# A decoder kernel's last microseconds: the final reciprocal root through ScalarE's square root, sums as one group, the last rows stored by column halves

## The chip, the core and the metric

The kernel runs on one core of a Trainium2 chip. The metric is the device time of one execution in microseconds (us); the value that counts is the median of several runs. Five engines work side by side, each through its own instructions in order: PE (TensorE, matrix products and transposes), DVE (VectorE), ACT (ScalarE), POOL (GpSimd) and SP (SyncE, which here only issues transfers). They wait for one another through semaphores. PE writes to PSUM, from which ACT and DVE read; the DMA engines carry data between SBUF and device memory.

## The reference

Two layers of a decoder trunk over 512 tokens of width 1024, in float32: layer 0 has a diagonal state-space mixer, layer 1 a short gated convolution, and each is followed by a SwiGLU feed-forward block of hidden width 2816. The end, which the change is about, is the last residual and a plain RMS norm:

```python
def rms_norm(x, g):
    x32 = x.astype(jnp.float32)
    y = x32 * lax.rsqrt(jnp.mean(x32 * x32, axis=-1, keepdims=True) + RMS_EPS)
    return (y * g.astype(jnp.float32)).astype(x.dtype)
...
        x = x + g2 * swiglu(h, w_ffn_in[i], w_ffn_out[i])
    return rms_norm(x, final_g)
```

## The kernel before

**Layout.** The activations stand transposed in `xT`: 128 partitions hold 128 of the 1024 channels, eight such blocks `k` lie side by side, and the free axis is the 512 tokens. Weights are split into a high part `wh` (rounded, copied by ACT) and a low part `wl` (the rest, by DVE or POOL), and every product is three matmuls: `wh` and `wl` by the high part of the activations, `wh` by the low part. The weights stream from device memory through SP's queue.

**Stages.** A state-space stage comes first (its instruction order is a table in the file), then the output projection of the mixer (`pre`, `half`, `glu`), the feed-forward block of layer 0, the convolution, the feed-forward block of layer 1, and the end. From the output projection on, the order is the order of the code, except that a scheduler moves an instruction forward on its engine when its operands and tiles are free early. In the output projection ACT and DVE turn the mixer's transposed result from PSUM (`ytp`) into the high and low parts `yT`, which `half` multiplies.

**The end.** The last product of layer 1 is done for the two halves of the tokens, `s=1` and then `s=2`, by `f1.tail`. For each half, `f1.fix` adds the residual into `xT` (DVE), squares it (ACT, `sq`) and adds the squares up over the channel blocks in `acc` (DVE); `fin_scale` multiplies by the final gain into `xg` (ACT); `fin_t` transposes `xg` back to rows of tokens in PSUM (`yt`, PE). `fin_sums` then sums `acc` over the partitions by matmuls against a column of ones (`ssq`, two row blocks `b` of 128 tokens) and calls `rsqrt_small`: an integer guess from the exponent and three Newton steps, 11 small DVE instructions on two columns of the tile `nst`. `fin_out` scales the rows by the result into `yo`: the left 512 columns on ACT, the right 512 on DVE; row block 0 is stored through SP's queue and row block 1 through ACT's, 512 KB each. For `s=1` all of this lies in `hook`, between the products of `s=2`; for `s=2` it is the end of the program. The last square of `s=2` isn't added into `acc`: it is summed by its own matmuls (`q`).

`rsqrt_small` is also used by the norms between the layers (`Norm.sums`).

Of the kernel before, what the change touches and what calls it, by code (L numbers as in the profile page):

```python
# [8 lines left out]
F32 = mybir.dt.float32  # L9
F32R = mybir.dt.float32r  # L10
I32 = mybir.dt.int32
AF = mybir.ActivationFunctionType
ALU = mybir.AluOpType
# [3 lines left out]
P = 128  # L17
D = 1024
# [7 lines left out]
EPS = 1e-6  # L26
# [235 lines left out]
def rsqrt_small(e, n, src, scale):  # L262

    h, y, t = e.nst[:, 0, 0:n], e.nst[:, 1, 0:n], e.nst[:, 2, 0:n]
    e.ts(h, src, scale / 2, EPS / 2, ALU.mult, ALU.add)
    e.ts(y.bitcast(I32), h.bitcast(I32), -0.5, float(0x5F3759DF - 0x80400000), ALU.mult, ALU.add)
    for _ in range(3):
        for c in range(n):
            q = slice(c, c + 1)
            e.stt(t[:, q], y[:, q], y[:, q], h[:, q], ALU.mult, ALU.mult)  # L270
        e.stt(y, t, 1.5, y, ALU.subtract, ALU.mult)
    return y


@with_exitstack
def hybrid_trunk(ctx: ExitStack, tc, x, c, norm1_g, norm2_g, w_ada, b_ada,
# [3 lines left out]
    e = common(tc, ctx)  # L280
    nc = tc.nc
    V, A, PE, SP = e.V, e.A, e.PE, e.SP
# [48 lines left out]
    SL = (slice(0, T), slice(0, TH), slice(TH, T))  # L331
# [39 lines left out]
    if 1:  # L371
# [35 lines left out]
        fp = ctx.enter_context(tc.tile_pool(name="fp", bufs=2))  # L407
        ws.wx = ctx.enter_context(tc.tile_pool(name="wx", bufs=Weights.EXTRA))

        def ft(tag, n=T, dt=F32):  # L410
            return fp.tile([P, n], dt, tag=tag, name=tag)

        accs = fp.tile([P, T], F32, tag="acc", bufs=1, name="acc")
# [21 lines left out]
        class Norm:  # L435
# [5 lines left out]
            def sums(self):  # L441
                self.ps = e.ps("ssq")
                o = (self.s - 1) * TH
                for b in range(2):
                    e.mm(self.ps[:, b:b + 1], accs[:, o + b * P:o + b * P + P], e.ones1[:, 0:1], True, True)
                self.y = rsqrt_small(e, 2, self.ps[:, 0:2], 1.0 / D)
# [238 lines left out]
        ov = out[0].rearrange("(c h j) d -> h c j d", h=2, j=4)  # L685
# [3 lines left out]
        def fin_scale(k, s):  # L689
            A.activation(out=rows(xg[s][:, k]), in_=rowsin(xT[:, k, SL[s]]), func=AF.Copy, scale=e.vec2[:, 24 + k:25 + k])  # L690
# [9 lines left out]
        def fin_out(n, s):  # L700
            for b in range(2):
                yo = e.slot([P, D], "yo")
                A.activation(out=yo[:, 0:512], in_=yt[(s, b, 0)], func=AF.Copy, scale=n.y[:, b:b + 1])
                V.tensor_scalar_mul(out=yo[:, 512:1024], in0=yt[(s, b, 1)], scalar1=n.y[:, b:b + 1])
                (SP if b == 0 else A).dma_start(out=ov[s - 1, b * 32:b * 32 + 32], in_=yo)

        def fin_sums(s, q=None):

            ps = e.ps("ssq")
            for b in range(2):  # L710
                cs = slice(b * P, b * P + P)
                e.mm(ps[:, b:b + 1], accs[:, SL[s]][:, cs], e.ones1[:, 0:1], True, q is None)
                if q is not None:
                    e.mm(ps[:, b:b + 1], q[:, cs], e.ones1[:, 0:1], False, True)
            n = Env()
            n.y = rsqrt_small(e, 2, ps[:, 0:2], 1.0 / D)
            return n

        for k in range(4):
            for s in (1, 2):  # L720
                fin_scale(k, s)
# [6 lines left out]
        def hook(j):  # L728
            if j == 0:
                n1.append(fin_sums(1))  # L730
                fin_t(1, range(KD))
            if j < 3:
                f1.fix(j, t2, 2)
                fin_scale(4 + j, 2)
            if j == 2:
                fin_out(n1[0], 1)
# [4 lines left out]
        q = ft("sq")[:, 0:TH]  # L741
        A.activation(out=rows(q), in_=rowsin(xT[:, 7, SL[2]]), func=AF.Square)
        fin_scale(7, 2)
        fin_t(2, range(7))
        n2 = fin_sums(2, q)
        fin_t(2, [7])
        fin_out(n2, 2)


# [745 lines left out]
```

## Time and profile before

| | |
|---|---|
| median of three runs | 1159.06 us (1158.73 to 1160.02) |
| the profiled execution | 1159.56 us |
| its span, first to last instruction | 1157.8 us |
| mean granted clock of PE | 0.986 |
| PE busy | 1105.8 us (96% of the span) |
| DVE busy | 643.7 us (56%) |
| ACT busy | 390.3 us (34%) |
| POOL busy | 180.7 us (16%) |

The 1.8 us between the span and the execution's own time lie before the first and behind the last instruction. The terms of the prediction are taken from the profiled execution; it is 0.5 us above the median.

In the timeline a row is: start in us, length in us, engine, line, operation, what is written from what, count, and in brackets how long the engine sat idle before it and who ended that. Rows of equal instructions that follow each other are merged; the length then runs from the first start to the last end. `SPq` and `ACTq` are what SP's and ACT's sequencers do, such as issuing a transfer. In the chain of work a row is start, length and work; `issue` is time for which nothing in the profile shows a cause.

### The profile page before, as it was taken

Reading aid. Unit: us, or ns where it says so; the run is one execution under the profiler, and the core shown is the slowest. Engines: PE = TensorE matmul, PEld = TensorE weight load, DVE = VectorE, ACT = ScalarE, POOL = GpSimd, SP = SyncE. Lnnn points to the kernel's source line nnn. Section 1 sums busy time; section 2 is a strip of 40 time slices with the busy share of each in tenths; the row PEclk is TensorE's granted clock in tenths of the full one; section 3 lists DMA queues with packets and bytes.
Section 4 is the critical chain, followed back from the end, with each engine's and each line's share of the span. In section 5 each row is a group of like instructions: output and inputs, shape, how many; then the busy total and the mean of one; then the engine's idle time right before and its main releaser. Section 6 shows DMA issues by size and latency. Waiting matters only on the chain.

```text
span 1157.8 us, 16329 instructions
## 1 busy us (share of the span) xinstructions
PE 1105.8 (96%) x6520; PEld 932.5 (81%) x6520; DVE 643.7 (56%) x1249; ACT 390.3 (34%) x596; POOL 180.7 (16%) x134
## 2 busy tenths in 40 slices
PE   4778999899999999999999999999999999999997
PEld 2567778898888888888889888899888888888886
DVE  8898323974666267734687666757334324243234
ACT  4744344442231132222334242334223113222244
POOL 4897817400000000000050000031000000000000
PEclk9889999899999999999999999999999999999999
DMA  9337654217894498726723939512332332332101
GB/s 280 126 115 259 201 184 128 91 55 182 194 195 120 119 194 196 182 91 137 173 92 100 207 113 209 154 58 89 110 110 80 103 109 78 104 109 92 63 28 73
DMA packets 141787, 153.50 MB, mean 133 GB/s; under 512 B 8224, under 2 KB 129164, under 8 KB 141712
## 3 DMA queue, kind: packets, MB, share of 16 engines
q1 hardware_dynamic: 140640, 150.79, 48.7%
q10 hardware_dynamic: 784, 1.58, 0.5%
q8 instruction: 51, 0.84, 0.3%
q0 software_dynamic: 288, 0.10, 0.1%
q14 instruction: 24, 0.20, 0.1%
HBM read 147.99 MB, written 2.10 MB: 130 GB/s over the span
## 4 chain that ended last, share of the span: by engine, by line
PE 85%; DVE 11%; ACT 2%; issue 1%; DMA 0%; DVEq 0%; ACTq 0%
PE o L117 79%; PE t L117 2%; DVE sx L109 1%; DVE scq L109 1%; DVE sg L109 1%; DVE hlo L115 1%; DVE xT L115 1%; PE gmm L117 1%; DVE acc L109 1%; PE yps L117 1%; DVE sr L120 0%; DVE v L109 0%; PE xtp L118 0%; ACT u L1229 0%; DVE scr L115 0%
## 5 line engine op out<-in xcount | busy, mean ns | idle before, releaser
L117 PE MATMUL o<-wide,wh 128*128 128x512 f32 (+1 forms) x992 | 364.2, 370 | 1.8 <-ACT wide L459 1.8
L117 PE MATMUL o<-wide,wl 128*128 128x512 f32 (+1 forms) x992 | 363.4, 369 | 0.0
L117 PE MATMUL o<-hlo,wh 128*128 128x512 f32 (+1 forms) x992 | 354.7, 370 | 2.3 <-DVE hlo L115 2.2
L119 ACT ACTIVATE wh<-wr 128x1024 fp32r<-128x1024 f32 (+1 forms) x184 | 188.6, 1039 | 387.0 <-PE o L117 305.1
L109 DVE TENSOR_TENSOR wl<-wr,wh 128x1024 fp32r<-128x1024 f32 (+1 forms) x156 | 184.8, 1195 | 157.8 <-ACT wh L119 156.0
L117 PEld LDWEIGHTS o<-wide,wh 128*128 128x128 f32 x992 | 187.6, 189 | 33.4 <-ACT wide L459 2.6
L117 PEld LDWEIGHTS o<-wide,wl 128*128 128x128 f32 x992 | 187.5, 189 | 30.8
L117 PEld LDWEIGHTS o<-hlo,wh 128*128 128x128 f32 x992 | 182.8, 189 | 34.8 <-DVE hlo L115 3.1
L117 PE MATMUL o<-hid,wh 128*128 128x512 f32 (+1 forms) x704 | 205.5, 375 | 0.0
L109 POOL TENSOR_TENSOR wl<-wr,wh 128x1024 fp32r<-128x1024 f32 x28 | 68.5, 2464 | 571.4 <-ACT wh L119 561.6
L117 PEld LDWEIGHTS o<-hid,wh 128*128 128x128 f32 x704 | 129.2, 188 | 23.8
L117 PE MATMUL o<-hid,wl 128*128 128x512 f32 (+1 forms) x352 | 131.8, 375 | 0.0
L109 DVE TENSOR_TENSOR sg<-sg,o 128x512 f32<-128x512 f32 (+1 forms) x50 | 31.8, 644 | 166.5 <-PE o L117 163.7
L115 DVE SCALAR_TENSOR_TENSOR aacc<-ada,cper,aacc 128x256 f32<-128x256 f32 x217 | 108.3, 499 | 19.1 <-DMA ada<-in_w_ada_dram 13.2
L515 ACT ACTIVATE sg<-o 128x512 f32<-128x512 f32 (+1 forms) x48 | 26.8, 562 | 170.0 <-PE o L117 168.4
L117 PEld LDWEIGHTS o<-hid,wl 128*128 128x128 f32 x352 | 66.3, 188 | 11.8
L117 PE MATMUL o<-yT,wh 128*128 128x512 f32 (+1 forms) x256 | 72.9, 366 | 0.0
L115 DVE SCALAR_TENSOR_TENSOR xT<-o,mod,xT 128x512 f32<-128x512 f32 (+1 forms) x56 | 38.6, 692 | 55.0 <-PE o L117 54.7
L117 PEld LDWEIGHTS o<-yT,wh 128*128 128x128 f32 x256 | 46.1, 189 | 8.1 <-issue 0.4
L117 PE MATMUL o<-yT,wl 128*128 128x512 f32 (+1 forms) x128 | 46.4, 363 | 0.0
L429 ACT ACTIVATE sq<-xT 128x256 f32<-128x256 f32 (+1 forms) x43 | 23.5, 550 | 50.8 <-DVE xT L115 47.3
L109 DVE TENSOR_TENSOR acc<-acc,sq 128x256 f32<-128x256 f32 (+1 forms) x40 | 26.1, 652 | 17.4 <-ACT sq L429 17.2
(222 smaller groups left out, 1031.4 us busy)
## 6 DMA issues: line engine op xcount, KB each, us to landing
wr<-in_w_ffn_in_dram SPq DMA_DIRECT2D x88, 512.0 KB, 3.6
ada<-in_w_ada_dram SPq DMA_DIRECT2D x112, 256.0 KB, 9.6
wr<-in_w_ffn_out_dram SPq DMA_DIRECT2D x40, 512.0 KB, 3.9
gt<-in_w_ada_dram SPq DMA_DIRECT2D x12, 1024.0 KB, 6.0
wr<-in_conv_w_in_dram SPq DMA_DIRECT2D x24, 512.0 KB, 3.6
aw<-in_w_ada_dram SPq DMA_DIRECT2D x16, 512.0 KB, 8.6
wr<-in_ssm_w_out_dram SPq DMA_DIRECT2D x16, 512.0 KB, 6.3
wr<-in_conv_w_out_dram SPq DMA_DIRECT2D x8, 512.0 KB, 6.1
```

Source lines behind the costliest of these rows:

```text
L109: (eng or e.V).tensor_tensor(out=out, in0=a, in1=b, op=op)
L115: e.stt = lambda o, a, s, b, op0, op1: e.V.scalar_tensor_tensor(out=o, in0=a, scalar=s, in1=b, op0=op0, op1=op1)
L117: e.mm = lambda o, l, r, start, stop: e.PE.matmul(out=o, lhsT=l, rhs=r, start=start, stop=stop)
L119: e.cp = lambda o, i: e.A.activation(out=o, in_=i, func=AF.Copy)
L429: A.activation(out=rows(q) if st.get("rows") else q, in_=rowsin(xT[:, k, SL[s]]) if st.get("rows") else xT[:, k, SL[s]], func=AF.Square)
L515: A.activation(out=w, in_=g[:, 0:width(s)], func=AF.Silu)
```

## The change

`fin_sums` calls a new function, `rsqrt_root`, in place of `rsqrt_small`. ACT takes the square root of the mean square plus epsilon, DVE computes `-(mean + eps)/2` and the reciprocal of ACT's root, and one Newton step of three DVE instructions follows. In the matmuls of the sums, the two row blocks form one accumulation group, and the order is both blocks of `acc`, then both of `q`. For `s=2` each row block leaves in two transfers of 256 KB: the left columns through ACT's queue, the right ones through SP's. At the start of the end's code a tile `eps` of one column is filled by DVE, and ACT takes one square root of it, into a spare column of `nst`.

```diff
+def rsqrt_root(e, n, src, scale):
+    h, y, t = e.nst[:, 0, 0:n], e.nst[:, 1, 0:n], e.nst[:, 2, 0:n]
+    e.A.activation(out=t, in_=src, func=AF.Sqrt, scale=scale, bias=e.eps)
+    e.ts(h, src, -scale / 2, -EPS / 2, ALU.mult, ALU.add)
+    e.V.reciprocal(out=y, in_=t)
+    for c in range(n):
+        q = slice(c, c + 1)
+        e.stt(t[:, q], y[:, q], y[:, q], h[:, q], ALU.mult, ALU.mult)
+    e.stt(y, t, 1.5, y, ALU.add, ALU.mult)
+    return y
...
-                (SP if b == 0 else A).dma_start(out=ov[s - 1, b * 32:b * 32 + 32], in_=yo)
+                if s == 1:
+                    (SP if b == 0 else A).dma_start(out=ov[s - 1, b * 32:b * 32 + 32], in_=yo)
+                else:
+                    for h, q in enumerate((A, SP)):
+                        hs = slice(h * 512, h * 512 + 512)
+                        q.dma_start(out=ov[s - 1, b * 32:b * 32 + 32, :, hs], in_=yo[:, hs])
 
         def fin_sums(s, q=None):
 
             ps = e.ps("ssq")
-            for b in range(2):
-                cs = slice(b * P, b * P + P)
-                e.mm(ps[:, b:b + 1], accs[:, SL[s]][:, cs], e.ones1[:, 0:1], True, q is None)
-                if q is not None:
-                    e.mm(ps[:, b:b + 1], q[:, cs], e.ones1[:, 0:1], False, True)
+            qs = [accs[:, SL[s]]] + ([] if q is None else [q])
+            for i, t in enumerate(qs):
+                for b in range(2):
+                    e.mm(ps[:, b:b + 1], t[:, b * P:b * P + P], e.ones1[:, 0:1], i + b == 0, i + b == len(qs))
             n = Env()
-            n.y = rsqrt_small(e, 2, ps[:, 0:2], 1.0 / D)
+            n.y = rsqrt_root(e, 2, ps[:, 0:2], 1.0 / D)
             return n
 
+        e.eps = fp.tile([P, 1], F32, tag="eps", bufs=1, name="eps")
+        V.memset(e.eps, EPS)
+        A.activation(out=e.nst[:, 2, 4:5], in_=e.eps, func=AF.Sqrt)
```

The scheduler moves the two instructions that fill `eps` and take its root. On ACT in the output projection of layer 0, far ahead of the end, stands before (`wh` and `wl` are weights, `yT` the mixer's result, `part` a partial product, `sg` the gate):

```order
131 L119 ACTIVATE wh_2108<-wr_2094 128x1024
132 L119 ACTIVATE wh_2086<-wr_2084 128x1024
133 L119 ACTIVATE yT_1981<-ytp 128x2x256 x2
134 L119 ACTIVATE part_2044<-o_1880 128x512
135 L119 ACTIVATE wh_2114<-wr_2100 128x1024
136 L119 ACTIVATE wh_2120<-wr_2106 128x1024
137 L119 ACTIVATE wh_2126<-wr_2112 128x1024
138 L572 ACT_TABLE_LOAD
139 L572 ACTIVATE sg<-o_1998 128x512
```

and now:

```order
131 L119 ACTIVATE wh_2108<-wr_2094 128x1024
132 L119 ACTIVATE wh_2086<-wr_2084 128x1024
133 L739 ACT_TABLE_LOAD
134 L739 ACTIVATE nst<-eps 128x1
135 L119 ACTIVATE yT_1981<-ytp 128x2x256 x2
136 L119 ACTIVATE part_2044<-o_1880 128x512
137 L119 ACTIVATE wh_2114<-wr_2100 128x1024
138 L119 ACTIVATE wh_2120<-wr_2106 128x1024
139 L119 ACTIVATE wh_2126<-wr_2112 128x1024
140 L586 ACT_TABLE_LOAD
141 L586 ACTIVATE sg<-o_1998 128x512
```

The root of `eps` and a load of the function table that it needs stand ahead of the two copies to `yT`; the load for the gate's function behind them was there before.

On PE, at the same place, stand in both kernels the last products by the first half of `yT` and the first ones by the part that these two copies write:

```order
471 L117 MATMUL o_1999<-yT_1447,wl_1898 128x512
472 L117 MATMUL o_1999<-yT_1448,wh_1897 128x512
473 L117 MATMUL o_1996<-yT_1981,wh_2086 128x512
474 L117 MATMUL o_1997<-yT_1981,wh_2086 128x512
475 L117 MATMUL o_1998<-yT_1981,wh_2096 128x512
```

Nothing moved here; the first row with `yT_1981` waits for the second copy on ACT.

At the end of the program, DVE has before, from the last residual on:

```order
890 L115 SCALAR_TENSOR_TENSOR xT<-t_9363,mod_87,xT 128x256
891 L116 TENSOR_SCALAR nst<-ssq 128x2
892 L116 TENSOR_SCALAR nst<-nst 128x2
893 L115 SCALAR_TENSOR_TENSOR nst<-nst 128x1 x2
894 L115 SCALAR_TENSOR_TENSOR nst<-nst 128x2
895 L115 SCALAR_TENSOR_TENSOR nst<-nst 128x1 x2
896 L115 SCALAR_TENSOR_TENSOR nst<-nst 128x2
897 L115 SCALAR_TENSOR_TENSOR nst<-nst 128x1 x2
898 L115 SCALAR_TENSOR_TENSOR nst<-nst 128x2
899 L704 TENSOR_SCALAR yo<-yt,nst 128x512 x2
```

and now:

```order
887 L115 SCALAR_TENSOR_TENSOR xT<-t_9366,mod_87,xT 128x256
888 L116 TENSOR_SCALAR nst<-ssq 128x2
889 L281 RECIPROCAL nst<-nst 128x2
890 L115 SCALAR_TENSOR_TENSOR nst<-nst 128x1 x2
891 L115 SCALAR_TENSOR_TENSOR nst<-nst 128x2
892 L718 TENSOR_SCALAR yo<-yt,nst 128x512 x2
```

Five instructions stand where eleven stood, and the first of them, `-(mean + eps)/2`, now waits for ACT's root of the same sums, not for the sums alone.

On ACT, in the midst of the products of `s=2`, stands now, where before the row with `xg_9254` was followed by `sq`:

```order
468 L704 ACTIVATE xg_9254<-xT,vec_76 128x4x64
469 L279 ACT_TABLE_LOAD
470 L279 ACTIVATE nst<-ssq,eps 128x2
471 L443 ACTIVATE sq<-xT 128x4x64
472 L704 ACTIVATE xg_9255<-xT,vec_76 128x4x64
473 L717 ACTIVATE yo<-yt,nst 128x512 x2
474 L720 DMA out_dram<-yo 32x4x1024
```

A second load of the table stands ahead of the root of `s=1`, although the root of `eps` was taken earlier. The last rows on ACT are now:

```order
479 L763 ACTIVATE sq<-xT 128x4x64
480 L704 ACTIVATE xg_9255<-xT,vec_76 128x4x64
481 L279 ACTIVATE nst<-ssq,eps 128x2
482 L717 ACTIVATE yo<-yt,nst 128x512 x2
483 L724 DMA out_dram<-yo 32x4x512 x2
```

The root of `s=2` has no load ahead of it, and both of ACT's transfers stand behind both of its scalings; SP issues the other two, each when DVE's half is ready.

## The prediction

> **What bounds the kernel now.** I read the chain of waits first, since it says which engine sets the end; then its end, instruction by instruction, beside the timeline of the last microseconds; then the DMA share of those microseconds; and last, because the order puts a new instruction there, the output projection at 175 us. From the profile's page:
>
> ```profile
> PE 85%; DVE 11%; ACT 2%; issue 1%; DMA 0%; DVEq 0%; ACTq 0%
> ...
> L902 DVE RECIPROCAL scr<-scr 128x32 f32<-128x32 f32 x1 | 0.3, 347 | 0.0
> L871 ACT ACTIVATE cvec<-cps 128x8 f32<-128x8 f32 x1 | 0.2, 177 | 0.0
> L1074 ACT ACTIVATE co<-pw 128x32 f32<-128x32 f32 x1 | 0.2, 229 | 0.0
> L115 DVE SCALAR_TENSOR_TENSOR scr<-scr 128x32 f32<-128x32 f32 x34 | 4.7, 183 | 0.1
> ```
>
> PE carries 85% of the chain, so what delays PE delays the end. The four rows below it, from the groups of instructions, are prices used further down. The change's own stage is short. The chain there and the timeline of its instructions:
>
> ```profile
> 1138.03 0.34 PE ssq L117 x4
> ...
> 1140.17 6.47 PE t L117 x54
> 1146.64 1.53 PE yt L118 x14
> 1148.17 0.80 PE ssq L117 x8
> 1149.00 0.17 DVE nst L116
> ```
>
> ```profile
> 1147.72 0.72 ACT L690 ACTIVATE xg<-xT,vec 128x256 f32<-128x256 f32 x1
> ...
> 1149.00 0.16 DVE L116 TENSOR_SCALAR nst<-ssq 128x2 f32<-128x2 f32 x1 [1.83 <-PE ssq L117]
> 1149.19 0.17 DVE L116 TENSOR_SCALAR nst<-nst 128x2 int32<-128x2 int32 x1
> 1149.40 1.70 DVE L115 SCALAR_TENSOR_TENSOR nst<-nst 128x1 f32<-128x1 f32 x9
> 1151.19 1.26 ACT L703 ACTIVATE yo<-yt,nst 128x512 f32<-128x512 f32 x2 [2.75 <-DVE nst L115]
> 1151.20 1.41 DVE L704 TENSOR_SCALAR yo<-yt,nst 128x512 f32<-128x512 f32 x2
> 1152.03 0.57 SPq L705 DMA_DIRECT2D out_dram<-yo  x1
> 1152.70 0.59 ACTq L705 DMA_DIRECT2D out_dram<-yo  x1
> ```
>
> From the end of the sums (1148.17 + 0.80) to the end of the root (1149.40 + 1.70) DVE runs eleven tiny instructions with nothing beside them: 2.13 us, all on the path. Then the scalings take 1.41 us, and the rest is the two stores. Their traffic, from the table of stretches (columns: stretch, length, busy time of PE, its loads, DVE, ACT, POOL, then clock, DMA share and GB/s); the last row is an early stretch whose loads have 2 KB rows:
>
> ```profile
> 1153.00:1153.25 0.25, 0.00 (x0) 0.00 (x0) 0.00 (x0) 0.00 (x0) 0.00 (x0) 1.00 0.00 0
> 1153.25:1155.75 2.50, 0.00 (x0) 0.00 (x0) 0.00 (x0) 0.00 (x0) 0.00 (x0) 0.54 1.02 406
> 1155.75:1156.00 0.25, 0.00 (x0) 0.00 (x0) 0.00 (x0) 0.00 (x0) 0.00 (x0) 0.50 0.37 131
> ...
> 15.00:23.00 8.00, 8.00 (x68) 5.13 (x71) 7.59 (x56) 2.63 (x13) 0.00 (x0) 1.00 1.05 386
> ```
>
> The first bytes move at 1153.25, 1.22 us after the first issue; from then on all 16 DMA engines are full at 406 GB/s until about 1155.84. The second store never waits for anything but the first one's bytes.
>
> **The root (on the path).** It removes 2.13 us. In its place ACT takes the root of two columns from PSUM. The nearest rows are 177 ns (8 columns from PSUM) and 229 ns (32 columns from SBUF); I take 0.20. ACT is free by then: its `xg` ends at 1148.44, and the order puts no table load here. Then follow, each on DVE: `h`, which by the order waits for ACT's root, 0.16 as the row at 1149.00; the reciprocal; and three steps of the kind of which nine took 1.70, 0.57 with their gaps. The reciprocal took 347 ns for 32 columns where a plain instruction of that size took 183; the excess is 5 ns a column, so two columns should cost 0.17, and 0.35 is the ceiling. A handover takes the 0.03 from 1148.97 to 1149.00; three of them are 0.08. Sum 0.20 + 0.16 + 0.17 + 0.57 + 0.08 = 1.18. The gain is 2.13 - 1.18 = 0.95, and 0.74 with the dear reciprocal and the dear root, and 1.15 if ACT's root cost nothing.
>
> **The sums.** Eight PE instructions of 0.10 us before (two for each product), eight now, in another order. The last square stands on ACT ahead of the `xg` of 1147.72, so it is ready before the transposes end (1146.64 + 1.53), and neither order waits for it: 0, within 0.1 either way.
>
> **The stores.** The bytes are the same, in 2 KB rows instead of 4 KB. At 386 instead of 406 GB/s the 1.05 MB take 2.72 us instead of 2.59: +0.13. Against this, the first transfer no longer needs both engines' halves: ACT's left half of block 0 is ready 0.68 us after the scaling starts (half of 1.26 and an overlap), the SP store of before went 0.84 after. Whether ACT's sequencer can issue while its second scaling runs, this stretch shows:
>
> ```profile
> 115.57 1.06 ACT L119 ACTIVATE wh<-wr 128x1024 fp32r<-128x1024 f32 x1 [1.77 <-DVE scq L109]
> 115.59 2.53 ACTq L1355 DMA_DIRECT2D wide<-kr  x2
> 118.17 0.60 ACT L119 ACTIVATE xT<-xtp 128x512 f32<-128x512 f32 x1 [1.54 <-issue]
> ```
>
> It can: two issues start while ACT computes, and only what stands behind them waits (until 118.17). So the first issue comes 0.13 earlier, the four end at about 0.7, 0.83, 1.3 and 1.5 us plus 0.6, and the later ones are in line before the engines run dry. Sum about 0; bounds -0.15 and +0.5, the latter if ACT's two issues of 0.59 go one behind the other after both scalings and the flow has a gap.
>
> **The root of `s=1` (hidden).** Two rows of ACT around it:
>
> ```profile
> 1136.94 0.72 ACT L690 ACTIVATE xg<-xT,vec 128x256 f32<-128x256 f32 x1
> ...
> 1141.11 1.26 ACT L703 ACTIVATE yo<-yt,nst 128x512 f32<-128x512 f32 x2 [1.27 <-DVE nst L115]
> ```
>
> ACT is free from 1137.66, so the load (1.28, below) ends at about 1139.0 and the root at 1139.2, 0.8 us after the sums (1138.37). DVE's `h` starts that much later, but six DVE instructions fewer follow, so the scaling starts near 1140.7 where it started at 1141.1. What it must free, the PSUM of the first transposes, PE needs at 1146.64; PE's 54 products from 1140.17 depend on none of it. Cost 0; the cover is four microseconds, and if it went, the load's 1.28 would show.
>
> **The early root of `eps` (a stall).** Here the order counts. Rows of ACT, DVE and PE at that place, the stretch of the chain that contains it, and the nearest table load:
>
> ```profile
> 173.93 1.06 ACT L119 ACTIVATE wh<-wr 128x1024 fp32r<-128x1024 f32 x1 [4.21 <-PE gmc L118]
> 174.89 1.07 ACT L119 ACTIVATE yT<-ytp 128x512 fp32r<-128x512 f32 x2
> 175.85 0.60 ACT L119 ACTIVATE part<-o 128x512 f32<-128x512 f32 x1
> 174.14 0.06 DVE L618 MEMSET cv<- 128x2 f32 x1
> 175.50 1.29 DVE L109 TENSOR_TENSOR yT<-ytp,yT 128x512 fp32r<-128x512 f32 x2 [1.20 <-ACT yT L119]
> 177.00 1.07 PE L117 MATMUL o<-yT,wh 128*128 128x512 f32 x4
> ...
> 174.64 24.52 PE o L117 x108
> 199.18 1.06 ACT wh L119
> ```
>
> ```profile
> 183.08 1.06 ACT L119 ACTIVATE wh<-wr 128x1024 fp32r<-128x1024 f32 x1 [1.25 <-DMA wr<-in_ssm_w_out_dram]
> 184.16 1.28 ACT L572 ACT_TABLE_LOAD   x1
> 185.46 0.60 ACT L572 ACTIVATE sg<-o 128x512 f32<-128x512 f32 x1
> ```
>
> ACT's copy `wh` ends at 174.99. From the end of a copy (184.14) to the start behind a load (185.46) it is 1.32 us, so the root of `eps` starts at 176.31 (its memset is done at about 174.2) and, at 0.20, ends at 176.51. The two copies to `yT` then start 0.10 before that, as they now overlap their forerunner, and end at 177.48 instead of 175.96. PE's last product by the old `yT` is the first of the four at 177.00, which start 0.227 apart (24.52 us for 108); the next, at 177.23, waits for the second copy. It is late by 0.25, and 0.04 for the handover: a stall of 0.29 us. The chain runs through PE here from 174.64 to 199.16 without a gap, and the ACT copy behind it waits for PE, so nothing takes it back. DVE's low parts end 1.52 later too, at 178.3, and by the order PE uses them eleven products after the first, at 179.7. The bounds: 0 if PE comes to that product 0.3 later than its modelled start, 0.6 if the small root has a start-up of 0.3 that no row shows.
>
> The Trainium skill, "ScalarE: Activation LUTs", section "What ACT_TABLE_LOAD costs", counts about 1.28 us for the load and 1.38 us for a drain, 2.66 us for every switch. The load's 1.28 agrees with the row above; the drain does not, since 1.32 us lie between the copy and the next function. By the skill's page, as an estimate, the stall would be 1.63 instead of 0.29 and the sum +0.7 instead of -0.7.
>
> **The sum.** -0.95 (root) + 0 (sums) + 0 (stores) + 0 (`s=1`) + 0.29 (stall) = -0.66 us on an execution of 1159.56 us: 1158.90. That execution is 0.50 above the median of 1159.06, so for the median I forecast 1158.4. Runs of the kernel before lie 1.3 us apart; 0.2%, 2.3 us, is about what a measurement can tell from no change here, so the forecast is: no change that can be told.
>
> **Rivals.**
>
> 1. *The stall costs more than the end gains: slower.* The mechanism is ACT's queue at 175 us: two copies to `yT` stand behind the load, and PE behind them. The slack is 177.23 - 175.96 = 1.27 us; the rows put 1.52 there. From 2.22 us of inserted work on (1.27 + 0.95) the change loses. With a load twice as long as the row's, 2.56 in place of 1.28, the stall is 1.57 and the median 1159.06 - 0.95 + 1.57 = 1159.7. For it speaks only that the row at 184.16 sits where ACT has little behind it; against it, the exact length. Chance 0.10. The 2.66 us of the Trainium skill's page named above would bring this case about.
> 2. *The stall is hidden.* If PE's modelled times or the copies leave 0.3 us more, only the end counts: 1159.06 - 0.95 = 1158.1. Chance 0.20.
> 3. *The four stores drain one behind the other on each queue.* The stores of before landed 3.1 (SP) and 3.7 us (ACT) after issue. If a queue's second store began only when its first had landed, the last would land 0.83 + 3.1 + 3.1 = 7.0 us after the scaling's start, where it was 1.5 + 3.7 = 5.2: +1.8, and the median 1160.2. The full DMA share from 1153.25 on, with two stores in flight, speaks against it. Chance 0.06.
>
> ```profile
> out_dram<-yo SPq DMA_DIRECT2D x2, 512.0 KB, 3.1
> out_dram<-yo ACTq DMA_DIRECT2D x2, 512.0 KB, 3.7
> ```
>
> 4. *The root does not get shorter.* If ACT's part takes a microsecond by a start-up that no row shows, the end gains nothing and the stall stays: 1159.06 + 0.29 = 1159.4. The small ACT rows of 177 to 229 ns speak against it. Chance 0.06.
>
> The forecast itself keeps 0.51, with its own range of 1157.7 to 1159.1. What is left, 0.07, is for something beyond 2.3 us that no row shows: 0.03 faster, 0.04 slower. All the others lie within 0.2% of before, so "the same" has 0.93. For the range, 1157.3 to 1160.1 takes in the forecast and rivals 1, 2 and 4 with the half microsecond by which a median of few runs moves; it leaves out rival 3 and the rest.
>
> **What would show it.** Right: two more table loads on ACT, near 175 and 1138 us; a gap of about 0.3 us before PE's first product by the new `yT`; at the end ACT's root, then five DVE instructions, some 1.2 us from the sums to the scalings; a DMA share that stays near 1 for 2.6 to 2.7 us and starts no later after the scaling than now. Wrong: a gap of more than a microsecond at 177 us, a root chain above 1.4 us, a hole in the DMA share of the last stores, or a wait of PE near 1146.6 for the scaled rows of `s=1`.

## Result and the profile after

The changed kernel takes 1167.55 us in the median of its runs (1166.70 to 1171.68), the kernel before 1159.38 us beside it: a ratio of 1.0074, interval 1.0061 to 1.0088. It is slower by some 8 us; the forecast was 1158.4 us, range 1157.3 to 1160.1. The profiled execution took 1167.06 us (span 1165.3 us, granted clock 0.988, before 0.986). Executions of one and the same kernel can lie some 7 us apart (the kernel before, in the runs beside e12: 1158.80 to 1166.02 us), so the causes below are read from the traces, row against row.

The places that the prediction looked at come first. The end, from the chain of waits (start, length, engine, what it writes) and the timeline (start, busy time, engine, line, operation, idle time before it):

```profile
1148.31 6.41 PE t L117 x54
1154.72 1.53 PE yt L118 x14
1156.25 0.80 PE ssq L117 x8
```

```profile
1157.08 0.26 ACT L279 ACTIVATE nst<-ssq,eps 128x2 f32<-128x2 f32 x1 [0.56 <-PE ssq L117]
1157.37 0.16 DVE L116 TENSOR_SCALAR nst<-ssq 128x2 f32<-128x2 f32 x1 [2.12 <-ACT nst L279]
1157.45 0.16 DVE L281 RECIPROCAL nst<-nst 128x2 f32<-128x2 f32 x1
1157.64 0.55 DVE L115 SCALAR_TENSOR_TENSOR nst<-nst 128x1 f32<-128x1 f32 x3
1158.22 1.27 ACT L717 ACTIVATE yo<-yt,nst 128x512 f32<-128x512 f32 x2 [0.88 <-DVE nst L115]
...
1158.94 1.28 ACTq L724 DMA_DIRECT2D out_dram<-yo  x2
1159.07 1.43 SPq L724 DMA_DIRECT2D out_dram<-yo  x2
```

The sums end at 1157.05 (8.08 us later than before), and ACT's scaling starts 1.17 us after them, where it was 2.22 us. So the root brought 1.05 us. From there to the end of the span it is 7.08 us, before 6.61: the stores took 0.47 us of it back. The traffic (columns as in the prediction):

```profile
1160.00:1160.25 0.25, 0.00 (x0) 0.00 (x0) 0.00 (x0) 0.00 (x0) 0.00 (x0) 1.00 0.16 57
1160.25:1162.75 2.50, 0.00 (x0) 0.00 (x0) 0.00 (x0) 0.00 (x0) 0.00 (x0) 0.71 1.02 379
1162.75:1163.00 0.25, 0.00 (x0) 0.00 (x0) 0.00 (x0) 0.00 (x0) 0.00 (x0) 0.50 0.89 320
1163.00:1163.25 0.25, 0.00 (x0) 0.00 (x0) 0.00 (x0) 0.00 (x0) 0.00 (x0) 0.50 0.11 33
```

379 instead of 406 GB/s makes the flow about 0.25 us longer, and the span ends about 2.27 us after the last byte instead of 1.96.

The place at 177 us, ACT, PE and PE's weight loads (`PEld`), and then the chain:

```profile
174.19 1.06 ACT L119 ACTIVATE wh<-wr 128x1024 fp32r<-128x1024 f32 x1 [3.94 <-PE gmc L118]
175.27 1.28 ACT L739 ACT_TABLE_LOAD   x1
176.56 0.20 ACT L739 ACTIVATE nst<-eps 128x1 f32<-128x1 f32 x1
176.67 1.07 ACT L119 ACTIVATE yT<-ytp 128x512 fp32r<-128x512 f32 x2
...
177.25 1.50 PE L117 MATMUL o<-yT,wh 128*128 128x512 f32 x4
...
177.79 0.53 PEld L117 LDWEIGHTS o<-yT,wh 128*128 128x128 f32 x3 [0.57 <-ACT yT L119]
```

```profile
174.19 1.06 ACT wh L119
175.27 1.28 ACT L739
176.67 1.08 ACT yT L119 x2
177.79 22.24 PE o L117 x96
```

The four products that took 1.07 us now take 1.50, and the chain passes through the table load: the stall is there, 0.4 us. Root, stores and stall together are -0.16 us. That is not where 8 us went.

They went to products of which the change edits nothing. Here is one block of 384 matmuls and one of 1584 in the chain of before, and then the same blocks after:

```profile
321.52 87.20 PE o L117 x384
...
794.45 341.42 PE o L117 x1584
```

```profile
323.21 87.88 PE o L117 x384
...
799.86 344.15 PE o L117 x1584
```

The same matmuls, without a gap between them, take 0.8% longer, at a granted clock no lower than before. So the loss in these blocks is no new wait; the matmuls themselves are dearer. In the trace a product has two records: PE loads the weights (`LDWEIGHTS`, 128x128), and the other operand, called moving here, goes through with its 512 columns (`MATMUL`). The tiles of the weights come from two pools of SBUF, `wp` and `wx`. Matching the starts of PE's records with the program's order tells which products are dearer. Between 246 and 1110 us the mean distance from one 512-column matmul to the next is, by the pool that holds the weights of both:

```
                               kernel before   changed kernel
both in wp (5 pairs of tiles)   226.80 ns       226.94 ns   (some 2300 matmuls)
both in wx (2 pairs of tiles)   226.78 ns       232.96 ns   (some 870)
from wp to wx                   227.4 ns        234.9 ns    (some 70)
from wx to wp                   227.3 ns        232.3 ns    (some 70)
```

Every 512-column matmul with weights from `wx` is about 6 ns dearer; step by step, after against before, that adds up to 6.5 us. What the change did to `wx` the diff does not show: `eps` is a new tile in `fp`, the pool opened just ahead of `wx`. Its 4 bytes in each partition take 32, and the weight tiles of `wx` begin at 207808 instead of 207776. No other tile has moved.

### The profile page after: what moved, and what is told of

Read it like the earlier page. It is cut to its first block, busy times and chain, and to the rows that moved or that the text cites. A ratio compares the mean times of both kernels' runs of the same rounds, so it can differ in the third digit from the quotient of the medians.

```text
span 1165.3 us, 16323 instructions
## 1 busy us (share of the span) xinstructions
PE 1112.3 (95%) x6520; PEld 931.4 (80%) x6520; DVE 642.1 (55%) x1238; ACT 393.7 (34%) x601; POOL 180.7 (16%) x134
## 4 chain that ended last, share of the span: by engine, by line
PE 80%; DVE 12%; DMA 3%; ACT 3%; issue 1%; SPq 0%; DVEq 0%; ACTq 0%
PE o L117 74%; DMA ada<-in_w_ada_dram 3%; PE t L117 2%; DVE sx L109 1%; DVE scq L109 1%; DVE sg L109 1%; DVE hlo L115 1%; DVE xT L115 1%; PE gmm L117 1%; DVE acc L109 1%; DVE aacc L115 1%; PE yps L117 1%; DVE wl L109 1%; DVE sr L120 0%; PE xtp L118 0%
```

## The experiments

Theory A: the place of these tiles costs the 6.5 us. Theory B: something else in the change does (the early root, the table loads, the new instructions). Each diff below is the whole edit of its kernel.

**e1: the kernel before, with nothing but the shift**

```
+ pad = fp.tile([P, 1], F32, tag="pad", bufs=1, name="pad")
+ V.memset(pad[:, 0:1], EPS)
```

> The kernel before, with one unused 4-byte tile in the pool fp and a memset of it; nothing of the change is in it. The two extra pairs of weight tiles (pool wx) lie 32 bytes further on: 207808 instead of 207776, so their place modulo 64 is 0 and no longer 32. Theory A (placement: matmuls that take their weights from the shifted tiles are slower, 6.2 ns each of 512 columns): +6 to +7 us, about 1166. Theory B (the change's instructions, the early root or the table loads slow PE): 0, about 1159.4. Theory C (two unlike programs differ by some us by chance): anything, and not in the matmuls with those weights.

Measured: 1166.58 us, ratio 1.0050 (1.0035 to 1.0065). With the kernel before otherwise as it was, the long block reads

```profile
799.18 344.15 PE o L117 x1584
```

which is the changed kernel's row to the hundredth; the spacing with `wx` is 232.96 ns. That is what theory A expects.

**e2: the whole change, without the shift**

```
- e.eps = fp.tile([P, 1], F32, tag="eps", bufs=1, name="eps")
+ e.eps = e.nst[:, 1, 7:8]
```

> The changed kernel, but eps lies in an unused column of the tile nst, so no tile is added and every weight tile lies where it lay in the kernel before. All instructions of the change remain. Theory A (placement): the 512-column matmuls are back at 226.8 ns; what remains is the change's own: -0.6 us at the end, +0.4 us at 177 us, and whatever part of the half microsecond near 745 us belongs to it: 1158.9 to 1159.8. Theory B (instructions): 1167.5. Theory C: between.

Measured: 1159.97 us where before had 1160.28; ratio 0.9999 (0.9983 to 1.0015), spacing 226.78 ns, the long block 341.41 us. The loss is gone. So is the stall at 177 us, which the expectation had left in: the order now puts the early root at 4.4 us. The load of the table at 3.09 us is there in the kernel before too, and ACT's next work, on the first tokens, waits for its data until 6.2 us in both:

```profile
3.09 1.28 ACT L739 ACT_TABLE_LOAD   x1 [3.09 <-DVE selh L120]
4.38 0.20 ACT L739 ACTIVATE nst<-nst 128x1 f32<-128x1 f32 x1
```

**e9: the whole change, the same order of instructions, another shift.** e2 had moved an instruction as well; this one does not.

```
- e.eps = fp.tile([P, 1], F32, tag="eps", bufs=1, name="eps")
+ e.eps = fp.tile([P, 64], F32, tag="eps", bufs=1, name="eps")[:, 0:1]
```

> The changed kernel, with the tile for eps made 64 columns wide (256 bytes) and only its first column used. Every instruction of the change stands in the same order on every engine; only the extra weight tiles lie 256 bytes further on than in the kernel before instead of 32. Theory A (placement, pattern of 256 bytes): matmuls at 226.8 ns, the stall at 177 us (0.4) and the end (-0.6) remain; about 0.2 us below before, 1159.2, or up to 0.7 above where the products by z wait near 745 us. Theory B (something else in the change costs): 1164 to 1167.

Measured: 1159.82 us beside 1159.75, ratio 1.0010 (0.9997 to 1.0022); spacing 226.77 ns. The stall at 177 us is there with 0.43 us. The same instructions in the same order, and only the place of four weight tiles differs: B falls.

```profile
794.87 341.41 PE o L117 x1584
```

**What about the place? e3, e6, e10 and e7** are e1 with `pad` 16, 32, 48 and 64 columns wide: a shift of 64, 128, 192 and 256 bytes.

> The kernel before, with a 64-byte pad instead of the 32-byte one: the extra weight tiles move twice as far, but lie at 32 modulo 64 as before. Theory A1 (it is the place modulo 64): 0, about 1159.4. Theory A2 (any shift of these tiles, or their place modulo 128 or more, counts): some microseconds, up to 1166.

> The kernel before, with a 128-byte pad: the extra weight tiles lie 128 bytes further on against everything else. If the pattern of the conflict repeats every 128 bytes: 226.8 ns for matmuls with those weights, 0 us. If it repeats at 256 or more: about 233 ns, +6 us.

> The kernel before, with a pad of 192 bytes. With a pattern of 256 bytes, 192 is 64 short of the next good place. If only the place itself is good: about 233 ns and +6 us, as at 32, 64 and 128. If the cost falls with the distance from a multiple of 256 on this side: less, 228 to 231 ns.

> The kernel before, with a 256-byte pad. If the pattern repeats every 256 bytes (before, the distance of these tiles from hid and from wide is a multiple of 256): 226.8 ns, 0 us. If it repeats at 512 or more, or not at all: about 233 ns, +6 us.

Measured, with the spacing of matmuls with `wx` weights:

```
shift, bytes    0 (before)  32 (e1)  64 (e3)  128 (e6)  192 (e10)  256 (e7)
spacing, ns       226.78    232.96   233.51    232.62    229.12     226.80
1584 matmuls, us  341.42    344.15   344.69    344.17    341.92     341.42
time, us         1159.38   1166.58  1166.60   1166.78   1160.15    1162.09
```

(The times of 0, 32 and 64 are medians; e3's ratio is 1.0050, 1.0033 to 1.0067.) A pattern that repeats every 32, 64 or 128 bytes is ruled out; at 256 the cost is gone. At 192 bytes, 64 short of that, a third of the cost is left between two `wx` products, and a fifth in the long block. e6, e10 and e7 have one time each, so here the rows of the traces carry the reading; e7's time is above before for another reason, told under e8.

**Place in memory, or place relative to something? e4 and e5.** In e4 all tiles of the kernel move by 32 bytes together; in e5 everything that is allocated behind `wide` does, while `wide` stays. `wide` and `hlo` hold the high and the low part of the input of a feed-forward block or of the convolution, `hid` the hidden values of a feed-forward block; all three are moving operands.

```
e4:  + e.cst.tile([P, 8], F32, name="pad")       ahead of e.ident
e5:  + e.cst.tile([P, 8], F32, name="pad")       behind e.wide
```

> The kernel before, with a 32-byte pad at the head of the first pool, so that all weight tiles and all moving operands move from 32 to 0 modulo 64 together. Theory A3 (weights at 0 modulo 64 are slow by themselves): every 512-column matmul becomes 6.2 ns dearer, about 4000 of them: +22 to +25 us, 1182. Theory A4 (weights and moving operand in unlike halves of 64 bytes are slow): 0, 1159.4, or a little faster if rows of 2 KB that begin at a 64-byte line are read in fewer lines. Theory B: 0.

> The kernel before, with a 32-byte pad right behind the tile wide: all weight tiles and all other moving operands (hid, hlo, z, yT) move 32 bytes together, and only wide, one of the moving operands, stays where it was. Theory A4 (what counts is where weights lie relative to the moving operand): 512-column matmuls with wide as the moving operand, about 1580 of them between 246 and 1110 us, become some 6 ns dearer with every weight tile, those with hid stay at 226.8 ns; +9 to +10 us, about 1169. Theory A5 (what counts is where the extra weight tiles lie relative to the other weight tiles, or absolutely): 0, about 1159.5.

Measured: e4 1159.27 us, ratio 1.0003 (0.9985 to 1.0021), spacing 226.81 ns with `wx` as with `wp`. So these addresses are not bad by themselves. e5 1175.15 us, ratio 1.0128 (1.0107 to 1.0150); its spacing by operand, and its group rows with those of before ahead of them (busy time, mean ns of one):

```
512-column matmuls, ns     wide,wh  wide,wl  hlo,wh  hid,wh  hid,wl
kernel before               226.9    226.5    227.1   226.9   226.3
e5                          233.8    234.9    231.2   226.8   226.6
```

```profile
L117 PE MATMUL o<-wide,wl 128*128 128x512 f32 x800 | 311.3, 389 | 0.0
L117 PE MATMUL o<-hid,wl 128*128 128x512 f32 x304 | 118.3, 389 | 0.0
```

```profile
L117 PE MATMUL o<-wide,wl 128*128 128x512 f32 x800 | 317.6, 397 | 0.0
L117 PE MATMUL o<-hid,wl 128*128 128x512 f32 x304 | 118.3, 389 | 0.0
```

Now it is the other way round: with all weight tiles, those of `wp` too, products of `wide` are slow, and those of `hid`, which moved along with the weights, are not. `wide` itself lies where it lay, and the weights lie as in e4, where they were fast. What counts is the distance between the weights and the moving operand; in the kernel before it is a multiple of 256 bytes for every pair. The size was a miss: 14 us, not 9 to 10, since the products of `hlo`, each between two of `wide`, became 4 ns dearer too, although `hlo` moved along with the weights; that their neighbours slow them is likely, but not shown.

**e8: rows instead of halves.** Is the 0.47 us at the end the column halves? e2 with the last rows stored as before:

```
- for h, q in enumerate((A, SP)):
-     hs = slice(h * 512, h * 512 + 512)
-     q.dma_start(out=ov[s - 1, b * 32:b * 32 + 32, :, hs], in_=yo[:, hs])
+ (SP if b == 0 else A).dma_start(out=ov[s - 1, b * 32:b * 32 + 32], in_=yo)
```

> The kernel of e2 (eps in an unused column of nst) with the last rows stored as before: one store of whole 4 KB rows from SP and one from ACT, no column halves. If the column halves cost what the profile of the changed kernel shows (from the start of the scaling to the end of the span 7.1 us with halves, 6.6 us with rows): 0.4 us less than e2. With the shorter root and no stall at 177 us the sum is -1.0 us against before: 1158.1 to 1158.5 where before is 1159.4. Rival (the halves cost nothing, the last microseconds vary between runs): the same as e2.

```profile
1151.95 1.26 ACT L717 ACTIVATE yo<-yt,nst 128x512 f32<-128x512 f32 x2 [0.88 <-DVE nst L115]
...
1152.85 0.56 SPq L719 DMA_DIRECT2D out_dram<-yo  x1
1153.52 0.58 ACTq L719 DMA_DIRECT2D out_dram<-yo  x1
```

From the scaling to the end of the span (1158.6) it is 6.65 us, in e2 7.03 (scaling at 1149.57, span 1156.6): the halves cost 0.4 us. The time is 1159.31 us where before has 1160.75, ratio 0.9991 (0.9982 to 1.0000). It has the lowest ratio of all versions, about a microsecond below before, but with an interval that reaches 1 it can't be told from no change.

Its profiled execution is no faster than that of before, and why is seen near 745 us, where PE waits for `z`, in e8 and in e7:

```profile
745.77 0.50 PE L117 MATMUL o<-z,wh 128*128 128x512 f32 x1 [0.38 <-ACT z L119]
746.85 0.73 PE L117 MATMUL o<-z,wh 128*128 128x512 f32 x2 [0.34 <-DVE z L109]
```

```profile
746.49 0.50 PE L117 MATMUL o<-z,wh 128*128 128x512 f32 x1 [1.51 <-ACT z L119]
747.56 0.73 PE L117 MATMUL o<-z,wh 128*128 128x512 f32 x2 [0.34 <-DVE z L109]
```

Against before, PE lost 1.3 us there in e8, 2.4 in e7, 1.0 in e3, 0.7 in the changed kernel, and nothing in e1, e2, e4, e5, e6, e9 and e10. DVE's work on `z` (the convolution's output, a moving operand) stands behind its steps on `ada`, the weights of the modulation that DVE sums up in `aacc`, and those steps wait for loads (total us, times, longest), in before and in e7:

```profile
DVE aacc L115 <- DMA ada<-in_w_ada_dram: 5.7, 3, 5.2
```

```profile
DVE aacc L115 <- DMA ada<-in_w_ada_dram: 8.0, 3, 5.7
```

Between 690 and 745 us these totals are 4.6 to 6.6 us in the traces in which PE lost nothing there, and 7.3, 7.6, 7.8 and 8.0 us in the changed kernel, e8, e3 and e7. So the loss goes with late loads, and a kernel with nothing but a pad has it too: it is not tied to the change. That the loads cause it, no edit has shown.

**e11 and e12: two attempts to take this wait away** from e8.

```
e11: - f0.body(rhs, 4)                       e12: - ada.step(16)    (behind conv_rest)
     + f0.body(rhs, 5)                            + ada.step(8)
                                                  - ada.finish()    (behind while ada.todo)
```

> The kernel of e8 (short root, eps in nst, whole rows), with 20 instead of 16 of VectorE's modulation steps after each group of the first feed-forward block, so that only 24 of the 64 steps that stood in the convolution remain there and its loads of ada fall by as many. The wait of PE for z near 745 us (0.7, 1.3 and 2.4 us in three traces, nothing in others, with VectorE waiting 5.5 to 8.0 us for loads of ada ahead of it) should go: 0 to 1.3 us less than e8, a median near 1158.3 where before is 1159.4. Rival: VectorE or the loads become too late inside the first feed-forward block (DMA share 0.65 there, VectorE busy 58%), and PE waits there instead: slower than e8 by some us.

> The kernel of e8, with 8 instead of 16 of VectorE's modulation steps after each of the four groups of the convolution (the 32 left over run after its output products, where steps of 16 stood without work), and without the call that finishes the last modulation right behind them (the next transition finishes it, some 15 us of PE's products later). Half of the ada loads of 700 to 720 us, where the DMA share is 1.15, move behind 745 us, where it is 0.32. If late ada loads cause PE's wait for z near 745 us: no such wait, runs closer together, 0 to 1.3 us less than e8: median 1158.2 to 1159 where before is 1159.4. Rival (the last steps or their loads now hold VectorE or PE in the transition near 770 us): some us slower than before.

Both missed. e11 takes 1217.12 us beside 1159.75, ratio 1.0493 (1.0477 to 1.0509). With steps of 20 a modulation ends in the middle of such a run of steps, and PE comes to the small product that closes it before DVE has accumulated its input. This wait alone is 49 of the 57 us:

```profile
L117 PE MATMUL adaps<-nsel,aacc 128*128 128x4 f32 x28 | 5.5, 302 | 49.1 <-DVE aacc L115 49.1
```

e12 takes 1162.91 us beside 1160.52, ratio 1.0016 (0.9994 to 1.0037), and PE loses 4.6 us near 745 us. The order did not move the steps back: loads and steps came forward into the same stretch (DMA share from 730 to 740 us 1.14, before 0.36), and steps now stand between DVE's instructions for `z`. How to take this wait away stays open; so does why the loads take longer in some executions.

## Why the prediction was wrong

- *The step that failed* is the count of what the early root of `eps` adds. The prediction costed the instruction, the table load and, as a time, the memset; the tile itself was not in the sum. It moved four weight tiles by 32 bytes and cost 6.5 us, where all the rest together is -0.16. The forecast's "something beyond 2.3 us that no row shows", at 0.04 for slower, is where this case fell; none of the signs that it named for being wrong came up.
- *The account* of the 8.08 us at the sums, trace against trace: 6.5 in matmuls with `wx`, 0.40 at 177 us, 0.7 in the wait for `z`, and 0.5 ahead of 240 us, where executions differ (at 240 us e10, with no part of the change, is 0.45 us earlier than before, and e8 0.5 later). Then -0.58 at the end: 7.5, the difference of the spans.
- *The root*: forecast 1.18 us from the sums to the scaling, measured 1.17. That it fits so well is in part luck: ACT's part was 0.26 instead of 0.20, and the reciprocal started 0.08 before `h` had ended, which the sum didn't have. The gain was 1.05 and not 0.95, because the forecast took the 1.18 up to the scaling from 2.13, which ends at the root's last instruction; up to the scaling it was 2.22. Rival 4 falls.
- *The sums*: 0.80 us for eight instructions, as before. Right.
- *The stores*: taken at 0, with +0.5 as a bound; measured +0.47 in the changed kernel and +0.4 by e8 against e2. The bound was right, the choice wrong: the flow took 0.25 us more, not 0.13, and the end after the last byte 0.3 more, for which the prediction had no term. The first byte did come earlier, by 0.1 us. A second store did not wait for the first to land (DMA share 1.02 from 1160.25 to 1162.75 us), so rival 3 falls.
- *The root of `s=1`*: hidden, as forecast. The load ran from 1145.82 to 1147.10, and PE went from its 54 products to the transposes of 1154.72 without a gap.
- *The stall*: forecast 0.29, measured 0.40 to 0.43 (changed kernel, e9). The mechanism is the one described, and the product that waited came 0.31 us late (177.79 instead of 177.25 + 0.23). The 0.1 that was missing comes behind it: the next product followed after 0.34 instead of 0.23 us, and PE's row of weight loads shows that the load of the waiting product waited for `yT` too. Rival 2, a hidden stall, falls with that; rival 1, a dearer one, falls because from the end of `wh` (175.25) to the root behind the load (176.56) it is 1.31 us. The change did come out slower, but not by rival 1's mechanism. The 2.66 us of the Trainium skill's page "ScalarE: Activation LUTs", section "What ACT_TABLE_LOAD costs", were not seen.
- *Sum without the missing term*: -1.05 + 0.47 + 0.42 = -0.16 us, and e9, without the shift, agrees: no change that can be told. The gain of the change was nearly eaten by its own two other parts; in e8, without either, about 1 us should remain, which its interval allows but doesn't show.

## What to carry to other kernels

When PE's products fill the time, compare the addresses of weights and moving operands before and after every edit that allocates anything, and keep their distances at a multiple that is known to be good (here 256 bytes): give a small constant a column in a tile that exists, or pad it. The sign of this fault is a chain with the same rows, no new wait and the same clock, in which long runs of the same matmuls have grown by a per cent or less; the spacing of their starts by weight tile then names the place. And a preload of an activation table is an instruction on ACT's queue like any other: see where the order puts it.

## What the runs showed of the hardware

- A 512-column fp32r matmul follows the one before it after 226.8 ns when weights and moving operand lie a multiple of 256 bytes apart, and after about 233 ns at 32, 64 or 128 bytes off, 229 at 192 (e1, e3, e6, e10, e7). Moving all together changes nothing (e4). The weight loads themselves last 188 to 189 ns in both cases, and products of 256 columns are no slower (122.8 ns with `wx`, before 124.2). Whether it is the weights in use or those being loaded meanwhile that count is not separated: in the changed kernel the step from a `wp` product to a `wx` product is slow already (234.9 ns), and the step back still is (232.3). That two reads of PE meet in memory would explain it, but no record shows the reads, so this remains argued.
- The Trainium skill, "SBUF — State Buffer", section "SBUF: two separate sides", says that on the engines' side only the port pair shared by VectorE and GpSimd causes contention and that PE never waits on anyone; in its table of paths PE's weight loads have a second, independent read port. The page speaks of engine against engine; within PE the place of the weights did matter here, by 6 ns in 227.
- In the kernel before whole 4 KB rows from two stores left at 406 GB/s, in the changed kernel column halves of 2 KB from four at 379, and the span ended 0.3 us later after the last byte. Which of the two, the length of the rows or the number of stores, makes the difference was not tried.
